# Writing both rounded parts of the residual state in permuted order, so that the gather's stationary chunks are contiguous columns

## The chip, the cores and the metric

The kernel runs on one core of one Trainium2 chip. The metric is the device time of one execution in microseconds (us). It is given as the median of several runs. One further execution was taken by the hardware profiler, and every row shown below comes from that one. The engines are named as the profile names them: PE is TensorE (PEld its weight loads), DVE is VectorE, ACT is ScalarE, POOL is GpSimd, and SP is the engine whose queue issues the weight transfers. A matmul has a stationary operand, which a weight load (LDWEIGHTS) puts into the array first, and a moving operand, which is then streamed through it.

## The reference, cut to what matters

One decoder layer on 256 tokens of width 2048: a norm, a projection, two kinds of attention, an output projection that is added to the residual state `h`, and then a mixture of 32 experts. Only the last part matters here.

```python
h = h + mixed @ w_out[layer]
hn = rms_norm(h, ffn_norm_w[layer])
h = h + hier_moe(hn, ...)

# hier_moe: a router picks 1 of 4 groups and 2 of its 8 experts for each token
for e in range(N_EXPERTS):                       # 32
    he = jax.nn.silu(xf @ w_gate[e]) * (xf @ w_up[e])
    y = y + combine[:, e:e + 1] * (he @ w_down[e])
```

Each expert has three float32 matrices of 4 MB (2048 x 512, 2048 x 512 and 512 x 2048).

## The kernel before

**The residual state.** `xs[t]` holds the state `h` as [128 tokens, 2048 columns] for token block t (0 or 1). For the expert stage it is split into two fp32r tensors, `hh[t][0]` (the rounded value) and `hh[t][1]` (what the rounding left). `split_h(n, eng)` makes columns 512 n to 512 n + 511 of them: two ACT copies (L872) and then two subtractions on the engine `eng` (L874). The first three chunks (n = 0, 1, 2) are split by DVE while the output projection `wo` still runs. The last one (n = 3) is split by POOL, called at L1083, while DVE works through the router's chain of small operations (L1090 to L1160), which ends in the one-hot matrix `s1` (L1065).

**Pairs of experts.** The 32 experts are taken as 16 pairs (`pr` 0 to 15). Each expert gets up to 64 tokens (`CAP`). `gather_j` picks the tokens of two pairs (four experts, 256 places) out of `hh` with matmuls: for chunk j of 512 columns, the stationary operand is a 128 x 128 piece of `hh` and the moving operand is the one-hot matrix `s1` of 256 columns. The weights of an expert are loaded so that partition p holds rows 4p to 4p + 3 of a chunk, so a gather needs for i = 0 to 3 the columns 4q + i of that chunk, q = 0 to 127. Before the change these are read with a step of four elements (16 bytes) out of `hh`, at L1197. One call of `gather_j` is 16 matmuls (4 values of i, 2 token blocks, 2 parts) into two PSUM tiles `bx`, and DVE takes each tile out at L1199 (`xg`).

**What runs when on PE.** The gather for pairs 0 and 1 stands ahead of the loop: chunks j = 0 and 1, then the gate matmuls `bg` of chunk 0, then chunk 2, `bg` of chunk 1, and so on. In the loop over pairs, an odd pair (1, 3, ..., 13) gathers for the next two pairs: a chunk of `gather_j` after each of the four parts of its `up` matmuls (`bu`, in `in_u`). So there are eight gathers of 4 x 16 = 64 matmuls. An even pair has none. After `bu` come the next pair's `bg` and this pair's `by` (down). Each part of `bg`, `bu` or `by` is 16 matmuls on two weight tiles.

**Weights.** All expert weights go through a ring of SBUF slots of 1 MB each: 391 loads in a fixed order on the SP queue (`expert_load`, L958). 20 slots are filled ahead of the expert stage, and in the stage 16 of them are reused in turn. A load waits until PE has finished with the tile that its slot held (`used(2)` after each part).

**The scatter.** `scatter_n` brings a pair's result back to the tokens, matmuls `bo`, and adds it to `y`. At the first pair (`base is None`) `y` is made from `hh`: DVE adds `hh[t][0]` to `bo` (L1280) and POOL adds `hh[t][1]` (L1281), eight times each. Later pairs add to `y` itself (L1283).

Of the kernel before, what the change touches and what calls it, by code (L numbers as in the profile page):

```python
# [11 lines left out]
F32 = mybir.dt.float32  # L12
# [4 lines left out]
ALU = mybir.AluOpType  # L17
# [4 lines left out]
P = 128  # L22
# [58 lines left out]
def tile_kernel(ctx: ExitStack, tc: tile.TileContext, a: dict, out):  # L81
    nc = tc.nc
    pe, act, dve, pool, sp = nc.tensor, nc.scalar, nc.vector, nc.gpsimd, nc.sync
# [26 lines left out]
    def m8(tag, name, shape, dt=F32):  # L110
        return big.tile([P, *shape], dt, tag=tag, name=name)

    def mm(o, l, r, start, stop):
        pe.matmul(o, l, r, start=start, stop=stop, skip_group_check=True)  # L114


    xs = [big.tile([P, D], F32, tag=f"s{t}", name=f"xs{t}") for t in range(2)]
# [746 lines left out]
    hh = []  # L864

    def split_h(n, eng):

        if not hh:
            hh.extend([m8(tag, f"hh{t}{k}", (D,), F32R) for k, tag in enumerate(HH[t])] for t in range(2))
        ns = slice(n * 512, (n + 1) * 512)  # L870
        for t in range(2):
            act.copy(hh[t][0][:, ns], xs[t][:, ns])  # L872
        for t in range(2):
            eng.tensor_tensor(hh[t][1][:, ns], xs[t][:, ns], hh[t][0][:, ns].bitcast(F32), ALU.subtract)  # L874


    def logits(n):
# [22 lines left out]
        if n < 3:  # L900
            yield
            split_h(n, dve)
            for _ in range(3):
                yield
# [72 lines left out]
    for i in range(4):  # L977
# [3 lines left out]
        for kk in range(4):  # L981
            k = 4 * i + kk
# [19 lines left out]
            hi, lo = halves[h]  # L1002
# [78 lines left out]
    act.copy(lgT[0:36, :], ob["lg"][0:36, :T])  # L1081
    act.copy(lgT[64:100, :], ob["lg"][64:100, :T])
    split_h(3, pool)  # L1083
    blg = bank("blt", "s")
    for t in range(2):
# [100 lines left out]
    def gather_j(nm_, xg, s1, j, n):  # L1186

        xt_ = mp.tile([P, 4, 4 * CAP], F32, tag="xg", name=f"xg{nm_}{j}", bufs=4)
        xg.append(xt_)
        m = n * CAP  # L1190
        per = 512 // m
        for i0 in range(0, 4, per):
            bx = psm.tile([P, 512], F32, tag="A", name=f"bx{nm_}{j}{i0}")
            for t in range(2):
                for k in range(2):
                    for i in range(i0, i0 + per):
                        mm(bx[:, (i - i0) * m:(i - i0 + 1) * m], hh[t][k][:, j * 512 + i:(j + 1) * 512:4],  # L1197
                           s1[:, t, 0:n].rearrange("p e c -> p (e c)"), i == i0 and t + k == 0, t + k == 2)
            dve.tensor_tensor(xt_[:, i0:i0 + per, 0:m], bx.rearrange("p (i s) -> p i s", i=per),  # L1199
                              fw[:, 4 * j + i0:4 * j + i0 + per].unsqueeze(2).broadcast_to([P, per, m]), ALU.mult)  # L1200
# [32 lines left out]
    hids, ys, y = [], [], []  # L1233
# [39 lines left out]
    def scatter_n(nm_, scT, n, base):  # L1273
        ns = slice(n * 512, (n + 1) * 512)
        for t in range(2):
            bo = psm.tile([P, 512], F32, tag="A", name=f"bo{nm_}{n}{t}")
            for k in range(2):
                mm(bo, scT[:, t * P:(t + 1) * P], ys[0][:, n % 2, k], k == 0, k == 1)
            if base is None:
                dve.tensor_tensor(y[t][:, ns], hh[t][0][:, ns].bitcast(F32), bo, ALU.add)  # L1280
                pool.tensor_tensor(y[t][:, ns], y[t][:, ns], hh[t][1][:, ns].bitcast(F32), ALU.add)  # L1281
            else:
                dve.tensor_tensor(y[t][:, ns], base[t][:, ns], bo, ALU.add)  # L1283

# [24 lines left out]
    xg = []  # L1309
    bgs = psm.tile([P, 512], F32, tag="GU", name="bg0")  # L1310
    gather_j("0", xg, s1, 0, 4)
    for j in range(4):
        if j < 3:
            gather_j("0", xg, s1, j + 1, 4)
        half_in("0", "g", xg, 0, lambda j, e: wt["g", 0, j, e], lambda: used(2), bgs, (j,))
# [3 lines left out]
    for pr in range(16):  # L1319
# [8 lines left out]
        def in_u(j):  # L1328

            if by is not None and j in (0, 2):  # L1330
                for n in (j, j + 1):
                    scatter_n(str(pr - 1), scT_, n, None if pr == 1 else y)
                if j == 0:
                    split_y(by, 2)
                    split_y(by, 3)
            if more:
                gather_j(str(pr + 1), xg2, s1, j, 4)
# [68 lines left out]
    with tc.If(over >= CAP + 1):  # L1406
        for r in range(1, T // CAP):
            with tc.For_i(0, 32, 2) as e0:
# [31 lines left out]
                for n in range(4):  # L1440
                    split_y(by, n)
                    scatter_n(nm_, scT, n, y)
# [42 lines left out]
```

## Time and profile before

| what | value |
|---|---|
| median of 3 runs | 1439.66 us (1438.49 to 1439.86) |
| the profiled execution: its own time | 1438.52 us |
| the profiled execution: span in the trace | 1436.7 us |
| PE busy | 1366.0 us, 95% of the span |
| DVE, ACT, POOL busy | 503.5, 311.0, 73.5 us |
| read from HBM | 476.63 MB |

The span goes from the first to the last instruction, and the execution's own time has 1.8 us more around it. A busy PE is not a PE at its peak: matmuls overlap one another, and the busy time counts the whole stretch that they cover.

### The profile page before, as it was taken

The numbers are of one execution on the slowest core, as the hardware profiler recorded it, in microseconds if no ns is written. First come the engines' busy times: TensorE is split into PE (matmuls) and PEld (weight loads), VectorE is DVE, ScalarE is ACT, GpSimd is POOL, SyncE is SP. The second block draws the span as 40 slices with busy tenths as digits, with TensorE's granted clock in tenths as the row PEclk, the third lists the DMA queues.
The fourth block names the chain that finished last, engine by engine and source line by source line (L and its number), as shares of the span: only waits on it lengthen the run. The fifth ranks groups of instructions, "written<-read, shape, count | busy, mean of one in ns | idle before, by whom it ended". The sixth has DMA issues, their size and how long they took to land.

```text
span 1436.7 us, 18318 instructions
## 1 busy us (share of the span) xinstructions
PE 1366.0 (95%) x7526; PEld 817.4 (57%) x7526; DVE 503.5 (35%) x1046; ACT 311.0 (22%) x632; POOL 73.5 (5%) x94
## 2 busy tenths in 40 slices
PE   9999999999999999999999998999899899899985
PEld 8999999899787635434434532633543353363332
DVE  4657877767765203013022120310302122031022
ACT  5454545545544000000000000010000000001003
POOL 0300010121100002000000000000000000000003
PEclk9999999999999999999999999999999999999998
DMA  8754344655695799899999999999999999999994
GB/s 274 223 170 146 121 139 129 200 161 164 229 354 210 301 398 408 350 421 421 421 420 421 421 421 421 421 420 421 420 420 421 420 422 420 422 421 421 421 400 153
DMA packets 116698, 480.04 MB, mean 334 GB/s; under 512 B 14368, under 2 KB 40832, under 8 KB 68352
## 3 DMA queue, kind: packets, MB, share of 16 engines
q1 hardware_dynamic: 112240, 474.53, 83.8%
q10 hardware_dynamic: 4368, 4.27, 0.9%
q8 instruction: 61, 1.00, 0.3%
q14 instruction: 29, 0.24, 0.1%
HBM read 476.63 MB, written 2.14 MB: 333 GB/s over the span
## 4 chain that ended last, share of the span: by engine, by line
PE 70%; DMA 22%; DVE 4%; ACT 2%; SPq 1%; issue 1%; ACTq 0%; POOL 0%; DVEq 0%; POOLq 0%
PE bu L114 12%; PE bg L114 10%; PE bx L114 9%; DMA e_d<-in_expert_w_down_dram 8%; DMA e_u<-in_expert_w_up_dram 8%; PE by L114 8%; PE fkv_ps L114 6%; PE wo L114 6%; DMA e_g<-in_expert_w_gate_dram 4%; PE bo L114 3%; PE q_ps L114 3%; PE fq_ps L114 3%; PE o L114 2%; PE kvw_ps L114 2%; PE kvs_ps L114 1%; PE s_n L114 1%
## 5 line engine op out<-in xcount | busy, mean ns | idle before, releaser
L114 PE MATMUL by<-e_d,hids 128*64 128x512 f32 (+2 forms) x1072 | 231.2, 575 | 16.0 <-DMA e_d<-in_expert_w_down_dram 15.3
L114 PE MATMUL bu<-e_u,xg 128*64 128x512 f32 x1024 | 237.2, 596 | 7.5 <-DMA e_u<-in_expert_w_up_dram 7.5
L114 PE MATMUL bg<-e_g,xg 128*64 128x512 f32 x1024 | 226.5, 594 | 0.0
L1271 DVE TENSOR_TENSOR ys<-by,ys 128x512 fp32r<-128x512 f32 x60 | 40.0, 687 | 418.3 <-ACT ys L1270 417.0
L114 PEld LDWEIGHTS by<-e_d,hids 128*64 128x64 f32 x1072 | 79.1, 137 | 163.4 <-issue 127.7
L114 PEld LDWEIGHTS bu<-e_u,xg 128*64 128x64 f32 x1024 | 71.9, 137 | 143.4 <-issue 126.1
L114 PEld LDWEIGHTS bg<-e_g,xg 128*64 128x64 f32 x1024 | 71.7, 137 | 133.8 <-issue 130.5
L114 PEld LDWEIGHTS bx<-s,hh 128*128 128x128 f32 x512 | 122.2, 330 | 23.6 <-issue 13.0
L114 PE MATMUL bx<-s,hh 128*128 128x256 f32 x512 | 128.4, 404 | 4.5 <-DVE y L1283 3.0
L1283 DVE TENSOR_TENSOR y<-y,bo 128x512 f32<-128x512 f32 x112 | 72.0, 684 | 144.2 <-PE bo L114 144.2
L1270 ACT CAST ys<-by 128x512 fp32r<-128x512 f32 x60 | 35.2, 586 | 289.7 <-PE by L114 182.8
L1199 DVE TENSOR_TENSOR xg<-bx,fw 128x512 f32<-128x512 f32 x64 | 44.3, 692 | 134.4 <-PE bx L114 134.4
L114 PE MATMUL bo<-ys,scT 128*128 128x512 f32 x240 | 73.0, 426 | 12.3 <-ACT ys L1270 6.2
L114 PE MATMUL wo<-cv_wo,ohi 128*128 128x512 f32 x256 | 80.6, 396 | 0.0
L114 PEld LDWEIGHTS bo<-ys,scT 128*128 128x128 f32 x240 | 38.0, 188 | 58.7 <-issue 41.5
L1213 ACT CAST scT<-bsc 128x256 fp32r<-128x256 f32 x16 | 6.0, 373 | 250.8 <-PE bsc L114 250.8
L114 PE MATMUL fkv_ps<-xhl,cv_fkv 128*128 128x256 f32 x384 | 59.7, 291 | 0.0
L114 PE MATMUL fkv_ps<-cv_fkv,xhl 128*128 128x256 f32 x384 | 56.3, 282 | 0.0
L1391 POOL TENSOR_TENSOR o<-y,e_fnw 128x256 f32<-128x256 f32 (+2 forms) x12 | 10.1, 868 | 840.9 <-DVE y L1304 840.9
L114 PEld LDWEIGHTS wo<-cv_wo,ohi 128*128 128x128 f32 x256 | 46.9, 188 | 10.4 <-issue 1.2
L188 DVE TENSOR_TENSOR cv_fkv<-raw_fkv,cv_fkv 128x1024 fp32r<-128x1024 f32 x32 | 42.7, 1335 | 28.7 <-ACT cv_fkv L187 28.7
L114 PE MATMUL fq_ps<-xhl,cv_fq 128*128 128x256 f32 x384 | 52.4, 289 | 0.0
(285 smaller groups left out, 1464.8 us busy)
## 6 DMA issues: line engine op xcount, KB each, us to landing
e_g<-in_expert_w_gate_dram SPq DMA_DIRECT2D x128, 1024.0 KB, 19.8
e_u<-in_expert_w_up_dram SPq DMA_DIRECT2D x128, 1024.0 KB, 19.7
e_d<-in_expert_w_down_dram SPq DMA_DIRECT2D x124, 1024.0 KB, 19.8
raw_fkv<-in_w_in_dram SPq DMA_DIRECT2D x32, 512.0 KB, 4.8
raw_wo<-in_w_out_dram SPq DMA_DIRECT2D x16, 1024.0 KB, 5.1
raw_q<-in_w_in_dram SPq DMA_DIRECT2D x8, 1024.0 KB, 5.2
raw_fq<-in_w_in_dram SPq DMA_DIRECT2D x8, 1024.0 KB, 5.0
raw_kvs<-in_w_in_dram SPq DMA_DIRECT2D x4, 1024.0 KB, 7.1
```

Source lines behind the costliest of these rows:

```text
L114: pe.matmul(o, l, r, start=start, stop=stop, skip_group_check=True)
L188: dve.tensor_tensor(lo, r, hi.bitcast(F32), ALU.subtract)
L1199: dve.tensor_tensor(xt_[:, i0:i0 + per, 0:m], bx.rearrange("p (i s) -> p i s", i=per), fw[:, 4 * j + i0:4 * j + i0 + per].unsqueeze(2).bro ...
L1213: act.copy(scT, bt[:, :T])
L1270: act.copy(hi, by[n])
L1271: dve.tensor_tensor(lo, by[n], hi.bitcast(F32), ALU.subtract)
L1283: dve.tensor_tensor(y[t][:, ns], base[t][:, ns], bo, ALU.add)
L1391: (dve if last else pool).tensor_tensor(o[t][:, ns], y[t][:, ns], fnw[:, ns], ALU.mult)
```

## The change

The change writes `hh` in another column order. Within each chunk of 512 columns, column 4q + i of the state goes to place 128 i + q. `split_h` therefore reads `xs` with a step of four elements and writes `hh` contiguously. The gather's stationary chunk i is then the 128 contiguous columns 128 i to 128 i + 127. Where `y` is first made from `hh`, at L1280 and L1281, the order is turned back: `y` and the PSUM tile `bo` are accessed with a step of four elements there, and `hh` contiguously. No instruction is added, removed or moved: on each engine the same instructions with the same sizes stand in the same order, and only the access patterns differ.

```diff
         ns = slice(n * 512, (n + 1) * 512)
-        for t in range(2):
-            act.copy(hh[t][0][:, ns], xs[t][:, ns])
-        for t in range(2):
-            eng.tensor_tensor(hh[t][1][:, ns], xs[t][:, ns], hh[t][0][:, ns].bitcast(F32), ALU.subtract)
+        src = [xs[t][:, ns].rearrange("p (q i) -> p i q", i=4) for t in range(2)]
+        for t in range(2):
+            act.copy(hh[t][0][:, ns].rearrange("p (i q) -> p i q", i=4), src[t])
+        for t in range(2):
+            eng.tensor_tensor(hh[t][1][:, ns].rearrange("p (i q) -> p i q", i=4), src[t],
+                              hh[t][0][:, ns].bitcast(F32).rearrange("p (i q) -> p i q", i=4), ALU.subtract)
...
-                        mm(bx[:, (i - i0) * m:(i - i0 + 1) * m], hh[t][k][:, j * 512 + i:(j + 1) * 512:4],
+                        mm(bx[:, (i - i0) * m:(i - i0 + 1) * m], hh[t][k][:, j * 512 + i * P:j * 512 + (i + 1) * P],
                            s1[:, t, 0:n].rearrange("p e c -> p (e c)"), i == i0 and t + k == 0, t + k == 2)
...
             if base is None:
-                dve.tensor_tensor(y[t][:, ns], hh[t][0][:, ns].bitcast(F32), bo, ALU.add)
-                pool.tensor_tensor(y[t][:, ns], y[t][:, ns], hh[t][1][:, ns].bitcast(F32), ALU.add)
+                hi, lo = (hh[t][k][:, ns].bitcast(F32).rearrange("p (i q) -> p i q", i=4) for k in range(2))
+                yp = y[t][:, ns].rearrange("p (q i) -> p i q", i=4)
+                dve.tensor_tensor(yp, hi, bo.rearrange("p (q i) -> p i q", i=4), ALU.add)
+                pool.tensor_tensor(yp, yp, lo, ALU.add)
```

## Rows read from the trace of the kernel before

**Rows 1.** The page: span, and the chain that ended last, by engine.

```profile
span 1436.7 us, 18318 instructions
...
PE 70%; DMA 22%; DVE 4%; ACT 2%; SPq 1%; issue 1%; ACTq 0%; POOL 0%; DVEq 0%; POOLq 0%
```

**Rows 2.** Windows: busy us (instructions) of each engine, clock, DMA share, GB/s.

```profile
core 0: us, PE busy (x) PEld busy (x) DVE busy (x) ACT busy (x) POOL busy (x), PEclk, DMA share, GB/s
476.00:524.00 48.00, 48.00 (x232) 21.77 (x233) 4.75 (x9) 3.43 (x7) 0.00 (x0) 1.00 0.80 314
524.00:572.00 48.00, 46.70 (x206) 23.56 (x203) 12.47 (x19) 3.03 (x5) 10.02 (x8) 1.00 1.01 421
572.00:592.00 20.00, 19.46 (x104) 9.64 (x102) 2.04 (x3) 1.46 (x5) 0.00 (x0) 1.00 0.71 270
592.00:1385.00 793.00, 752.82 (x3384) 325.21 (x3382) 151.55 (x231) 55.32 (x107) 0.00 (x0) 1.00 1.01 421
```

**Rows 3.** Waits of SP's queue, 476 to 592 us: total us, times, longest.

```profile
SPq L958 <- PE bg L114: 57.0, 10, 15.1
SPq L958 <- PE bu L114: 40.2, 8, 9.8
```

**Rows 4.** The chain in order of time: start us, us, what.

```profile
468.84 7.80 PE bx L114 x32
476.64 3.58 PE bg L114 x16
480.23 3.95 PE bx L114 x16
...
548.97 4.04 PE bx L114 x16
```

**Rows 5.** Weight loads by shape: busy us, mean ns of one, idle before.

```profile
L114 PEld LDWEIGHTS bx<-s,hh 128*128 128x128 f32 x512 | 122.2, 330 | 23.6 <-issue 13.0 <-DVE y L1283 8.1 <-DVE y L1280 1.4
...
L114 PEld LDWEIGHTS fkv_ps<-cv_fkv,xhl 128*128 128x128 f32 x384 | 50.5, 191 | 0.0
...
L893 PEld LDWEIGHTS bt<-cst,xs 128*128 128x128 f32 x32 | 4.9, 207 | 0.9 <-DVE xs L846 0.4
...
L283 PEld LDWEIGHTS xt<-cst,xs 128*128 128x128 f32 x32 | 3.7, 139 | 1.1 <-DVE xhl L285 0.9
```

**Rows 6.** Timeline of PE in the projection: start us, us, operation.

```profile
304.64 0.88 PE L114 MATMUL fkv_ps<-xhl,cv_fkv 128*128 128x256 f32 x6
305.36 0.88 PE L114 MATMUL fkv_ps<-cv_fkv,xhl 128*128 128x256 f32 x6
```

**Rows 7.** Windows again, with the granted clock in the third column from the right.

```profile
461.00:470.00 9.00, 5.86 (x46) 5.62 (x47) 7.15 (x38) 2.04 (x6) 2.49 (x2) 1.00 0.97 380
470.00:474.00 4.00, 4.00 (x19) 4.00 (x19) 1.38 (x2) 0.00 (x0) 0.00 (x0) 0.57 1.01 420
1360.00:1380.00 20.00, 15.65 (x68) 5.31 (x64) 2.62 (x4) 1.76 (x3) 0.00 (x0) 1.00 1.01 422
```

**Rows 8.** Timeline of POOL and DVE at the last split and the router.

```profile
462.21 2.49 POOL L874 TENSOR_TENSOR hh<-xs,hh 128x512 fp32r<-128x512 f32 x2 [1.70 <-ACT hh L872]
...
463.21 1.53 DVE L1100 TENSOR_TENSOR room<-room 128x64 f32<-128x64 f32 x2
...
465.16 0.30 DVE L1107 TENSOR_TENSOR room<-room 128x64 f32<-128x64 f32 x2
```

**Rows 9.** Timeline of POOL at three earlier places.

```profile
46.58 0.72 POOL L480 TENSOR_TENSOR bk<-kc,vec 128x240 f32<-128x240 f32 x1 [7.50 <-DVE kc L336]
...
52.05 4.13 POOL L480 TENSOR_TENSOR bk<-kc,vec 128x240 f32<-128x240 f32 x3 [0.20 <-DVE kc L336]
...
206.27 0.73 POOL L621 TENSOR_TENSOR sq<-sq,s 128x256 f32<-128x256 f32 x1
```

**Rows 10.** DVE and ACT groups by line: busy us, mean ns of one, idle before.

```profile
L1199 DVE TENSOR_TENSOR xg<-bx,fw 128x512 f32<-128x512 f32 x64 | 44.3, 692 | 134.4 <-PE bx L114 134.4
...
L1280 DVE TENSOR_TENSOR y<-hh,bo 128x512 f32<-128x512 f32 x8 | 5.1, 684 | 8.0 <-PE bo L114 8.0
...
L456 DVE TENSOR_TENSOR cb<-bcb,csf 128x120 f32<-128x120 f32 x4 | 0.9, 276 | 1.4 <-PE bcb L114 1.4
...
L872 ACT CAST hh<-xs 128x512 fp32r<-128x512 f32 x8 | 4.5, 611 | 0.0
```

## Prediction

> **What bounds the kernel now.** I read the page first, then windows by stage, then the waits of the load queue and the chain inside the stage that the change touches. The chain that ended last is 70% PE and 22% DMA [rows 1], so both kinds of stretch exist, and the question is in which one a saved microsecond counts. The windows answer it [rows 2]. From 592 to 1385 us the transfers run at 421 GB/s without a break. That is also the rate of the full stretch from 524 to 572 us, so it is the ceiling as this trace shows it. In those 793 us the kernel ends when its bytes have come, and PE time saved there only becomes waiting. Six of the eight gathers lie there.
>
> Before that the transfers are not full. From 476 to 524 us they run at 314 GB/s, and from 572 to 592 us at 270 GB/s [rows 2]. Measured against 421, the first stretch lacks 48 x (421 - 314) / 421 = 12.2 us of transfer, and the second 20 x (421 - 270) / 421 = 7.2 us. Together that is 19.4 us. The reader is to see who withholds them: the load queue waits for PE to give slots back, 57.0 us for `bg` and 40.2 us for `bu` [rows 3]. The first two gathers stand just there (468.84 to 491.7 us, and from 548.97 us on [rows 4]), and they delay each slot's release. So the first two gathers count, and only up to 19.4 us.
>
> **What a contiguous stationary operand is worth.** A weight load of the gather takes 330 ns, and the same shape and type with contiguous columns takes 191 ns in `fkv` [rows 5]. Another pair of rows isolates the step: the transposes of `xs` load 207 ns where they read every fourth column (`bt`) and 139 ns where they read contiguous ones (`xt`) [rows 5]. So I hold the step responsible, not the tensor. Spacing matters more than duration, because loads overlap matmuls. The gather's 512 loads cover 122.2 us without overlap, 239 ns each, and they set the pace. Six `fkv` matmuls with the same stationary and moving sizes start every 305.36 - 304.64 = 0.72 us [rows 6], 120 ns each. I take 119 ns saved per matmul, 1.9 us per call of 16, and 7.6 us per gather. The bounds: nothing, if something else holds the 239 ns, and 7.6 us.
>
> The Trainium skill's page "TensorE: Matmul & The Clock Gate", section "LDWEIGHTS (loading the stationary operand)", gives a load's time by the number of columns alone, for 128 columns about 107 ns; by it the step costs nothing and the sum would be zero. The trace disagrees, 330 against 191 ns [rows 5], so I give that rule little weight.
>
> **First gather.** Its two first calls run back to back, 32 matmuls in 7.80 us [rows 4]. From 470 to 474 us the mean granted clock is 0.57, so 1.2 GHz instead of 2.4 for 0.43 / 0.5 x 4 = 3.4 us, after a router stretch in which PE was busy 5.86 of 9 us [rows 7]. At half clock I double the 120 ns to 240, an estimate, no better than the 239 ns of now. So 3.4 / 0.239 = 14 matmuls gain nothing, and 18 x 0.119 = 2.1 us remain. If the half clock falls elsewhere next time, the two calls gain the full 3.8 us. The calls for j = 2 and 3 gain 1.9 us each. Slots are then freed 2.1, 4.0 and 5.9 us earlier, and from there to the next gather always 5.9 us earlier. The last starved moment of the first stretch lies behind all four calls, so the transfers get 5.9 of the lacking 12.2 us back (7.6 with the clock elsewhere).
>
> **Second gather.** Its four calls save 7.6 us again, on top of the 5.9 by which everything is early. The second stretch lacks only 7.2 us, so PE then frees slots before the queue needs them, and the 7.2 us go whole. From about 520 us on the transfers are full, and nothing further can be won: the remaining six gathers save some 45 us of PE time that turn into waits for transfers.
>
> **What the change may cost.** PSUM hand-over: DVE takes 0.69 us for each `bx` tile [rows 10], now about 1.9 us apart and then 0.96. There are two tiles, and I allow 0.4 us in the first gather for PE waiting on one; in the second it comes out of the 0.4 us by which 7.6 exceeds 7.2.
>
> POOL's last split is the edit that can reach the path. While its two subtractions run (462.21 to 464.70), two small DVE operations take 1.53 us that take 0.30 us elsewhere, and they end with POOL [rows 8]: DVE stands still until POOL is done, and the router's chain, on which the first gather waits, stands behind it. So any lengthening of these two operations moves the whole expert stage. POOL reads with a step here for the first time. Its nearest row is L480, which steps 16 elements in its source: 0.72 us for 240 elements, against 0.73 us for 256 contiguous ones [rows 9]. By that the step costs nothing. The worst L480 row is 4.13 / 3 = 1.38 us, beside DVE work. That is 1.9 times as long, which would add 0.9 x 2.49 = 2.3 us. I take 0.3 us, near the undisturbed row, and keep 0 and 2.3 as ends.
>
> The Trainium skill's page "GPSIMD Engine Reference", section "7. Performance pitfalls for Q7 kernels", says that reading SBUF with a byte step over 8 costs about half as much again. By that rule the two would take 1.2 us more and the sum would be 1.2 us worse; the undisturbed L480 row with its 64-byte step does not show it.
>
> The other edits I cost at nothing. The first six subtractions and six ACT copies of `split_h` lie beside `wo` matmuls on engines with idle time; the last ACT copies (611 ns, [rows 10]) start POOL, so a tenth more there is below 0.1 us. At L1280 DVE reads PSUM with a step; L456 reads it with a step of 16 elements and takes 276 ns for 120 elements, and L1280 takes 684 for 512 [rows 10], both close to 1 ns an element and a fixed part, so the step is free. If it doubled, eight times 0.68 = 5.4 us would stand in the second gather, less what its 7.6 us leave over. L1281's result is wanted only by the next pair's scatter.
>
> **Sum.** 5.9 + 7.2 - 0.4 - 0.3 = 12.4 us; for small stalls that I can't name I round to 12. The profiled execution took 1438.52 us (span 1436.7 [rows 1]), which gives 1426.5; it lies 1.14 us under the median of the runs, so the median after should be 1427.7. I say 1427.5.
>
> **Rivals.** (a) Hidden anyway: transfers at 421 GB/s bind, gain zero, 1439.7 us. For it speaks the long full stretch; against it the 19.4 us lacking before it, which wait for PE by name [rows 3]. 3%. (b) The change doesn't do what it says: the load's time hangs on columns alone (the rule above) or on the tensor, and the spacing stays at 239 ns; 1439.5 to 1442 with POOL's cost. Against it the two pairs of rows. 3%. (c) Partial: the spacing falls only half-way, say 180 ns, or POOL costs its 2.3 us. With 0.94 us saved per call, 1.1 + 1.9 + 3.8 less 0.7 give 6 us, 1433.5. 11%. (d) Slower: with PE faster, its waits for transfers grow by about 45 us, and PE falls to the half clock in them. A part of 16 matmuls then takes up to twice 3.58 us [rows 4], while its two tiles (2.1 MB) come in 5.0 us: each such part loses 2.2 us once no lead is left. Some 160 parts lie in the 793 us; one in ten at half clock would be 16 x 2.2 = 35 us against the 12, so about 1463. It decides from six such parts on. Against it: where PE waits for transfers today it is busy 15.65 of 20 us and the clock stays at 1.00, and the fall came after 5.86 of 9 us [rows 7]. 3%. My forecast keeps 80%.
>
> **How the numbers follow.** With the half clock elsewhere and POOL free the gain is 7.6 + 7.2 = 14.8 us, 1424.9, and the three runs of before spread by 1.4 us: I set 1423.5. The upper end takes in POOL's 2.3 us and most of (c): 1432.5. A measurement of this kernel can tell about 0.2%, 2.9 us, from no change. Faster: the forecast and (c) with little left out, 0.91. Slower: (d) and some of (b), 0.04. Same: the rest, 0.05.
>
> **What the profile after would show.** Weight loads of `bx` near 190 ns; a call of 16 in about 2.1 us instead of 3.95; the transfers at 421 GB/s from about 520 us on, with no second short stretch; the stretch 476 to 524 still short, but by about 6 us; SP's waits for `bg` and `bu` smaller there; more PE waiting for `e_d`, `e_u` and now `e_g` after 700 us with the clock at 1.00; POOL L874 near 1.27 us. A DMA rate that is broken again after 560 us, or POOL L874 at 2 us and more, would make the prediction wrong.

## Result, and the profile after

| kernel | median us | lowest to highest | ratio to before (95%) |
|---|---|---|---|
| before | 1439.08 (4 runs) | 1436.84 to 1439.86 | |
| after the change | 1427.58 (4 runs) | 1426.43 to 1428.56 | 0.9927 [0.9914, 0.9940] |

The change makes the kernel 11.5 us faster. Predicted were 1427.5 us and a gain of 12. The sum came out; some of its terms did not, and the rest of this document is about them. The profiled execution took 1427.72 us, 10.8 us less than the one of the kernel before. Below, "after" is this profile.

The page of the kernel after: its span and the chain that ended last, by engine, against [rows 1].

```profile
span 1425.9 us, 18327 instructions
...
PE 56%; DMA 37%; DVE 4%; ACT 2%; issue 1%; SPq 0%; ACTq 0%; POOL 0%; DVEq 0%; POOLq 0%
```

PE's share of the chain went from 70% to 56%, and DMA's from 22% to 37%: more of the end is now decided by transfers. The groups of the same profile (busy us, mean ns of one, idle before):

```profile
L114 PEld LDWEIGHTS bx<-s,hh 128*128 128x128 f32 x512 | 62.2, 188 | 23.8 <-issue 13.0 <-DVE y L1287 8.1 <-DVE y L1284 1.5
...
L1285 POOL TENSOR_TENSOR y<-y,hh 128x512 f32<-128x512 f32 x8 | 12.1, 1548 | 84.9 <-DVE y L1284 84.9
...
L873 ACT CAST hh<-xs 128x512 fp32r<-128x512 f32 x8 | 8.6, 1120 | 0.0
...
L1284 DVE TENSOR_TENSOR y<-hh,bo 128x512 f32<-128x512 f32 x8 | 7.9, 1080 | 7.5 <-PE bo L114 7.5
```

The weight load fell from 330 [rows 5] to 188 ns. The price stands in the other three rows: ACT's copy rose from 611 to 1120 ns and DVE's first scatter from 684 to 1080 ns [rows 10], and POOL's scatter rose by a fifth from what it was before:

```profile
L1281 POOL TENSOR_TENSOR y<-y,hh 128x512 f32<-128x512 f32 x8 | 10.0, 1288 | 95.9 <-DVE y L1280 95.9
```

The windows, against [rows 2], and one from the part that is bound by transfers:

```profile
core 0: us, PE busy (x) PEld busy (x) DVE busy (x) ACT busy (x) POOL busy (x), PEclk, DMA share, GB/s
476.00:524.00 48.00, 48.00 (x249) 18.98 (x250) 4.75 (x9) 3.43 (x7) 0.00 (x0) 1.00 0.94 368
524.00:572.00 48.00, 45.01 (x240) 20.84 (x238) 17.03 (x22) 3.91 (x9) 12.05 (x8) 1.00 1.01 422
572.00:592.00 20.00, 20.00 (x96) 6.94 (x94) 0.00 (x0) 1.27 (x2) 0.00 (x0) 1.00 0.97 382
592.00:1375.00 783.00, 711.35 (x3342) 288.61 (x3340) 150.45 (x231) 54.62 (x106) 0.00 (x0) 1.00 1.01 421
...
1350.00:1370.00 20.00, 15.65 (x66) 5.33 (x62) 3.07 (x5) 1.85 (x4) 0.00 (x0) 1.00 1.01 421
```

The first stretch now lacks 48 x (421 - 368) / 421 = 6.0 us of transfer instead of 12.2, and the second 20 x (421 - 382) / 421 = 1.9 instead of 7.2. Together 11.5 us came back: the gain in the medians, and 0.7 us more than the 10.8 between the two profiles. The second stretch is still broken, though; the prediction had named a broken rate after 560 us as a sign that it is wrong. From 592 us on nothing changed in the rate. SP's waits in the same two stretches (476 to 592 us) show whom this came from; [rows 3] had 57.0 and 40.2 (its waits for `by` rose, from 10.3 to 12.8 us):

```profile
SPq L960 <- PE bg L114: 50.4, 11, 11.5
SPq L960 <- PE bu L114: 36.7, 8, 8.7
```

The chain through the router and the first two gathers (start us, us, what), against [rows 4]. `room` is the scratch tile of DVE's small operations in the router.

```profile
465.44 2.51 DVE room L1102 x2
...
472.06 4.17 PE bx L114 x32
476.23 3.58 PE bg L114 x16
479.81 2.10 PE bx L114 x16
...
545.63 2.15 PE bx L114 x16
```

A call of 16 matmuls takes 2.10 us instead of 3.95. POOL's last split, which holds DVE at the router, against [rows 8]:

```profile
464.90 3.03 POOL L875 TENSOR_TENSOR hh<-xs,hh 128x512 fp32r<-128x512 f32 x2 [2.19 <-ACT hh L873]
...
465.40 2.55 DVE L1102 TENSOR_TENSOR room<-room 128x64 f32<-128x64 f32 x2
```

It takes 3.03 us instead of 2.49, and it starts later, because ACT's copies feed it.

One profile shows where the gain lies only when it is cut into pieces that both kernels share. `blt` is the router's matmul just ahead of POOL's split. All numbers are us, worked out from starts in the timelines of the two kernels and of a second run of the changed one (`c1_changed_again`, below).

| piece | before | after | c1 |
|---|---|---|---|
| start of the span to `blt` | 461.64 | 463.83 | 459.38 |
| `blt` to the first gather | 7.20 | 8.23 | 8.23 |
| first gather to the first `bu` | 31.42 | 24.10 | 26.21 |
| first `bu` to the end of the second gather | 78.28 | 72.30 | 72.32 |
| end of the second gather | 578.54 | 568.46 | 566.14 |

The first row is chance: c1 runs the same program as after and reaches `blt` 4.45 us earlier. By 460 us it had moved 88.9 MB and after 87.2 (added up from windows of 4 us), which is 4.0 us of transfer at 421 GB/s. The second row is a loss of 1.03 us by the change. The third is where the clock falls by chance, and the fourth is the steady part of the gain, 6.0 us.

### The profile page after: what moved, and what is told of

It is laid out like the page before. It is cut to its first block, busy times and chain, and to the rows that moved or that the text cites. A ratio compares the mean times of both kernels' runs of the same rounds, so it can differ in the third digit from the quotient of the medians.

```text
span 1425.9 us, 18327 instructions
## 1 busy us (share of the span) xinstructions
PE 1321.7 (93%) x7526; PEld 771.5 (54%) x7526; DVE 509.2 (36%) x1046; ACT 315.3 (22%) x632; POOL 75.9 (5%) x94
## 4 chain that ended last, share of the span: by engine, by line
PE 56%; DMA 37%; DVE 4%; ACT 2%; issue 1%; SPq 0%; ACTq 0%; POOL 0%; DVEq 0%; POOLq 0%
DMA e_u<-in_expert_w_up_dram 17%; DMA e_d<-in_expert_w_down_dram 17%; PE bu L114 12%; PE fkv_ps L114 6%; PE wo L114 6%; PE bg L114 4%; PE by L114 4%; PE bo L114 3%; PE q_ps L114 3%; PE fq_ps L114 3%; PE bx L114 3%; DMA e_g<-in_expert_w_gate_dram 3%; PE kcv_ps L114 2%; PE o L114 2%; PE kvw_ps L114 2%; PE kvs_ps L114 2%
## 5 line engine op out<-in xcount | busy, mean ns | idle before, releaser
L114 PE MATMUL bu<-e_u,xg 128*64 128x512 f32 x1024 | 243.9, 597 | 9.7 <-DMA e_u<-in_expert_w_up_dram 9.6
L114 PE MATMUL bg<-e_g,xg 128*64 128x512 f32 x1024 | 234.8, 596 | 12.9 <-DMA e_g<-in_expert_w_gate_dram 12.9
L114 PEld LDWEIGHTS bg<-e_g,xg 128*64 128x64 f32 x1024 | 81.7, 137 | 143.2 <-issue 107.0
L114 PEld LDWEIGHTS bu<-e_u,xg 128*64 128x64 f32 x1024 | 75.6, 136 | 148.3 <-issue 121.5
L114 PEld LDWEIGHTS bx<-s,hh 128*128 128x128 f32 x512 | 62.2, 188 | 23.8 <-issue 13.0
L114 PE MATMUL bx<-s,hh 128*128 128x256 f32 x512 | 68.7, 287 | 4.6 <-DVE y L1287 2.9
L1395 POOL TENSOR_TENSOR o<-y,e_fnw 128x256 f32<-128x256 f32 (+2 forms) x12 | 10.1, 866 | 835.9 <-DVE y L1308 835.9
L114 PEld LDWEIGHTS fkv_ps<-xhl,cv_fkv 128*128 128x128 f32 x384 | 50.3, 190 | 2.2 <-issue 1.2
```

What stands on the lines that cost most here:

```text
L1395: (dve if last else pool).tensor_tensor(o[t][:, ns], y[t][:, ns], fnw[:, ns], ALU.mult)
```

## Experiments

Theory at this point: the first two gathers pay for everything, and the edits at the edges (the splits and the first scatter) cost a few us each time. Rivals: the edges are free, or all eight gathers count. All kernels but the last were timed against the kernel before on the same chip.

**The gather alone.** Splits and scatter stay as before, and the gather reads contiguous columns. The tokens are thus gathered with their columns in another order than the weights expect.

```diff
-  mm(..., hh[t][k][:, j * 512 + i:(j + 1) * 512:4], ...)
+  mm(..., hh[t][k][:, j * 512 + i * P:j * 512 + (i + 1) * P], ...)
```

> Only the gather's stationary chunk is made contiguous; the splits and the first scatter are those of before. hh is not permuted, so the experts get the columns of each chunk in another order than their weights (this part of the computation is changed; the router and the amount of work are not). Theory: the gain lies in the first two gathers, and the stepped accesses of the change cost about 1.0 us at the last split (POOL and ACT, through DVE's stand) and 1.5 us at the first scatter. Without them this kernel gets 6 to 7.3 us back in the first stretch and all of the lacking 7.2 us in the second: 13 to 14.5 us under the kernel before, about 1425.5 us, so 2 us under the changed kernel. L1100's pair stays at 1.5 us. Rival, the stepped accesses cost nothing in the total: 1427.6 us, as the changed kernel.

Measured 1421.89 us, 0.9894 [0.9876, 0.9912]. That is more gain than the whole change gives (0.9928 in c1), so the edges cost about 5 us in the medians. The pieces show 1.0 us at the router (7.21 instead of 8.23) and 1.5 us in the second gather (70.81 instead of 72.30). Against c1 the first gather is shorter as well, 25.60 us instead of 26.21, and the three pieces make 3.1 us, as much as the two profiles' spans differ by (1423.5 and 1420.5 us). The rest is not placed; three of its four executions had a mean clock of 0.995 or 0.996, where the changed kernel's had 0.993 or 0.994, so some of it may be the clock.

**The edges alone.** The mirror image: splits and scatter as after the change, and the gather keeps its step of four. Again the gathered columns are in another order.

```diff
-  mm(..., hh[t][k][:, j * 512 + i * P:j * 512 + (i + 1) * P], ...)
+  mm(..., hh[t][k][:, j * 512 + i:(j + 1) * 512:4], ...)
```

> The splits and the first scatter of the changed kernel, with the stepped stationary chunk of before in every gather (the experts get the columns in another order, the work is the same). Theory: it pays the stepped accesses and gains nothing: 1.0 us later at the first gather, 1.5 us more in the second, both before the transfers are full, so about 2.5 us over the kernel before, 1441.6 us. Rival, the stepped accesses are free in the total: 1439.1 us. Third, the late start of 3.2 us seen after is all due to the change (not to a half clock in the first 20 us of that execution): 4.7 us over, 1443.8 us.

Measured 1439.64 us, 1.0016 [1.0007, 1.0024], a loss of 2.3 us. In its profile `blt` to the first gather takes 8.22 us and the second piece 80.09, against 7.20 and 78.28: 1.0 and 1.8 us. (Its clock was at 0.96 between 524 and 572 us, which is not priced here.) The chain has the gather at its old pace:

```profile
469.51 7.78 PE bx L114 x32
...
480.87 3.95 PE bx L114 x16
```

So the edges do not pay for anything by themselves, and the weight load does not get faster by the new layout alone. The interval's upper end is 1.0024 x 1437.81 - 1437.81 = 3.5 us, which leaves out the dearest of the three prices expected.

**The first two gathers contiguous, the last six stepped.** The six gather columns in another order.

```diff
+  near = nm_ in ("0", "2")
+  st = hh[t][k][:, j*512+i*P:j*512+(i+1)*P] if near else hh[t][k][:, j*512+i:(j+1)*512:4]
-  mm(..., hh[t][k][:, j * 512 + i * P:j * 512 + (i + 1) * P], ...)
+  mm(..., st, ...)
```

> The changed kernel with contiguous stationary chunks in the first two gathers alone; the other six step through hh as before (the experts from pair 4 on get the columns in another order, the work is the same). Theory: the six gathers lie where transfers at 421 GB/s bind, so the time is that of the changed kernel, 1427.6 us within 0.7. Rival, every gather counts alike, about 1.75 us each of 14 before costs: 2 x 1.75 less 2.5 us, so 1438 us.

Measured 1426.68 us, 0.9926 [0.9913, 0.9939]: the changed kernel's time. **The last six contiguous, the first two stepped** is the opposite (`not in`).

> The reverse: contiguous chunks in the last six gathers, stepped ones in the first two (the experts of pairs 0 to 3 get the columns in another order, the work is the same). Theory: no gain, only the cost of the stepped accesses, as in the kernel with the edges alone: about 2.5 us over the kernel before, 1441.6 us, although PE saves some 45 us. Rival, every gather counts alike: 6 x 1.75 less 2.5 us, so 8 us under, 1431 us.

Measured 1440.29 us, 1.0019 [1.0010, 1.0028]: no gain, and the edges' price stays. Two gathers of eight carry the whole gain. What the six do can be read from PE's waits for transfers (total us, times, longest); `e_g`, `e_u` and `e_d` are the weight tiles of gate, up and down. First the kernel with the first two contiguous, 592 to 1375 us:

```profile
PE by L114 <- DMA e_d<-in_expert_w_down_dram: 15.4, 13, 1.3
PE bu L114 <- DMA e_u<-in_expert_w_up_dram: 6.9, 6, 1.3
```

Then the kernel after, the same stretch:

```profile
PE by L114 <- DMA e_d<-in_expert_w_down_dram: 31.8, 24, 1.3
PE bg L114 <- DMA e_g<-in_expert_w_gate_dram: 12.9, 11, 1.3
PE bu L114 <- DMA e_u<-in_expert_w_up_dram: 9.6, 9, 1.3
```

22.3 us of waiting became 54.3, and in the windows of that stretch PE was busy 743.27 us in the one and 711.35 in the other, both with transfers at 421 GB/s. The same 32 us stand in both differences: PE time saved in the six gathers is waiting.

**The changed kernel again**, with the profile taken again, to see what of a profile is chance.

> The changed kernel again, unaltered, beside the three variants below. Ratio to the kernel before 0.992 to 0.993. From the router's blt matmul to the first gather 8.23 us again (7.20 in the kernel before). If the half clock of the first 20 us is by chance and not due to the change, this profile has it or not, with the router stage reached 2 us earlier when not.

Measured 1427.03 us, 0.9928 [0.9914, 0.9941]. Its windows and its chain at the first gather:

```profile
core 0: us, PE busy (x) PEld busy (x) DVE busy (x) ACT busy (x) POOL busy (x), PEclk, DMA share, GB/s
...
466.00:472.00 6.00, 4.63 (x23) 4.52 (x23) 3.56 (x14) 0.00 (x0) 0.00 (x0) 0.50 1.01 421
```

```profile
467.61 6.33 PE bx L114 x32
```

Here the granted clock was 0.50, that is 1.2 GHz, for about 5 of the 6.33 us that the first 32 matmuls took; after had the clock at 1.00 there and took 4.17. What a matmul takes at the low level can be read from the timeline of PE, cut at 469 and at 472 us:

```profile
468.63 5.31 PE L114 MATMUL bx<-s,hh 128*128 128x256 f32 x28
...
471.62 2.33 PE L114 MATMUL bx<-s,hh 128*128 128x256 f32 x14
```

Fourteen matmuls start in 471.62 - 468.63 = 2.99 us, 214 ns each. After had its low clock elsewhere: between 6 and 18 us its mean granted clock was 0.72, against 1.00 in c1.

**POOL's last split behind the router.** POOL's subtractions wait for the router's result, and so do not run beside DVE's chain; the last of the loads that the ring makes ahead move behind them.

```diff
-  split_h(3, pool)
+  split_h(3, pool, (0,))          # ACT's copies only
...
+  gone = mp.tile([P, 1], F32, tag="gone", name="gone", bufs=1)
+  pool.tensor_copy(gone, rc[:, 0, 0, 1:2])
+  split_h(3, pool, (1,))          # POOL's subtractions
```

> The changed kernel, but POOL's last subtractions start only when the router's chain on DVE is done (a one-element POOL copy that reads its last result stands ahead of them); the ring's last loads into xs follow them. Theory: the DVE operation that stood still beside POOL (L1102, 2.51 us for the pair) takes 0.3 us, so from blt to the first gather 6.0 us instead of 8.23, all slots come free 2.2 us earlier, and the total is 2.2 us under the changed kernel, 0.15% (the gather for j = 3 needs this part only 10 us later). Rival: DVE doesn't stand because of POOL, and nothing moves. Second rival: the two last loads into xs start about 3 us later and the gain is lost to the transfers.

Measured 1422.05 us, 0.9893 [0.9878, 0.9908]: some 5 us faster than the changed kernel, twice what was expected. DVE's chain and the first gather in its profile:

```profile
462.26 0.27 DVE room L1102 x2
...
466.69 4.15 PE bx L114 x32
```

The two `room` operations take 0.27 us instead of 2.51, and `blt` to the first gather falls from 8.23 to 6.03: that is 2.2 us, and it shows that POOL's split held DVE. The rest is about the clock. The timeline of PE in the same profile, at the router's last matmuls:

```profile
465.42 0.18 PE L114 MATMUL brk<-sel,lt 128*128 128x32 bf16 x1 [0.28 <-DVE sel L1146]
```

PE waits 0.28 us here; in the two profiles of the changed kernel it waits 2.48 and 2.46 us. The first 32 matmuls then ran at full clock, and the first gather took 24.02 us to the first `bu`, against 26.21 in c1. The mean clock of the runs is 0.995 to 0.996, against 0.993 and 0.994 for the changed kernel. A difference of 0.0025 over 1424 us at half speed is 0.0025 x 1424 / 0.5 = 7 us less at the low level in each execution, an estimate. c1 shows what such a stretch costs when it meets the first gather, 26.21 - 24.02 = 2.2 us. So 2.2 us are shown by the router's piece, and 2.2 more by the first gather of this pair of profiles; that the medians differ by the same cause is argued from the clock.

**The first `y` made ahead.** POOL makes `y` as the sum of the two parts of `hh` ahead of the first scatter, on time that it has to spare, and the first scatter then is like the later ones.

```diff
+  hi, lo = (hh[t][k][:, ns].bitcast(F32).rearrange("p (i q) -> p i q", i=4) for k in range(2))
+  pool.tensor_tensor(y[t][:, ns].rearrange("p (q i) -> p i q", i=4), hi, lo, ALU.add)
...
-  scatter_n(str(pr - 1), scT_, n, None if pr == 1 else y)
+  scatter_n(str(pr - 1), scT_, n, y)
```

> The changed kernel, but POOL adds the two parts into y ahead, while the first pair's down matmuls run, and the first scatter then adds bo to y like all others. Theory: the stepped DVE operation (1080 ns) at the first scatter was on PE's path, 1.5 us in all; the second gather gets them back: from the first bu to the end of the second gather 70.8 us instead of 72.3. The total gains up to 1.5 us, no more than the second stretch still lacks (1.8 us). Rival: the scatter is hidden, no difference.

Measured 1426.31 us, 0.9918 [0.9905, 0.9932]. The profile shows what was meant, 71.05 us from the first `bu` to the end of the second gather instead of 72.32. The ratios of this kernel and of c1 overlap, so its worth in time is not settled. **Both together:**

> Both of the edits above on the changed kernel. Theory: the gains add, 2.2 + 1.5 us: 3 to 4 us under the changed kernel, about 0.990 of the kernel before. Rival: either is hidden, then 2.2 or 1.5 us.

Measured 1423.94 us, 0.9905 [0.9890, 0.9920]. Not better than the split's move alone, and the intervals overlap. Whether the second edit adds anything on top of the first stays open.

**The clock by itself.** Ten more filler matmuls (L1089 of the changed kernel) keep PE busy through the wait at the router, after the change, and five more do so in the kernel before (17 to 22).

```diff
-  keep_clock("clock1", 17)
+  keep_clock("clock1", 27)
```

> The changed kernel with 27 instead of 17 dummy matmuls (their result is not used) beside the router's chain, so that PE is busy for 2.4 us more of the 2.5 us in which it waits for that chain. The first gather starts no sooner: 8.23 us after blt as before. Theory: with PE busy the clock stays at 2.4 GHz at the first gather in most executions, its first 32 matmuls take 4.1 us instead of up to 6.3, and the median is 1 to 2 us under the changed kernel, 1425 to 1426 us against about 1427; the remaining 3 to 4 us to the kernel with the split after the router are the earlier start (2.2 us) and chance. Rival: the clock plays no part, the split after the router gained its 5 us elsewhere, and this kernel takes 1427 us.

Measured 1424.84 us, 0.9918 [0.9904, 0.9931]. In its timeline PE's wait is gone, and in the chain the first 32 matmuls run at full pace:

```profile
467.61 0.18 PE L114 MATMUL brk<-sel,lt 128*128 128x32 bf16 x1 [0.23 <-DVE sel L1146]
```

```profile
468.88 4.15 PE bx L114 x32
```

But this execution had its low clock between 6 and 18 us (0.86), as after had, and after ran these matmuls at full pace without the filler. So this profile alone does not tell whether the filler did it, and in time it is 1.4 us against c1 with intervals that overlap. The profiles of all kernels together say more. In nine of them PE waits 1.46 to 2.48 us in front of `brk`, and eight of these have the low clock during the first gather; after is the ninth. In the other five (the two with filler and the three with the split moved) the wait is 0.23 to 0.35 us, and the clock is 1.00 there in all. What that is worth in the medians is not settled.

> The kernel before with 22 instead of 17 dummy matmuls at the same place (its router is 1 us shorter, so fewer fit). Theory: with stepped chunks a gather matmul takes 234 to 239 ns at either clock, so the clock at the first gather is worth nothing there: same as before within 0.1%. Rival: a half clock costs the kernel before as much as the changed one, then 1 to 2 us under before.

Measured 1436.36 us, 1.0000 [0.9989, 1.0010]. This profile has the clock at full around the router. The 32 matmuls take 7.75 us, against 7.80 [rows 4], and the first gather takes 31.36 us to the first `bu`, as it took 31.42 with the fall in it. So a stepped gather does not gain from the higher clock: 239 ns per matmul holds at either level.

**The split behind the router, again:**

> The changed kernel with POOL's last subtractions after the router's chain, unaltered from the earlier run. Ratio 0.988 to 0.991 to the kernel before again; from blt to the first gather 6.0 us, PE's wait for the router 0.3 us, and the first 32 gather matmuls in 4.1 us if the clock stays up.

Measured 1422.02 us, 0.9896 [0.9881, 0.9911]. It agrees with the first time. Its low clock fell at neither place, and the first gather took 24.08 us to the first `bu`. This version beats both kernels, the kernel before by 15 us.

**What a step costs, operand by operand** (one execution, for its profile). Chunk 1 of the splits reads contiguously and writes with a step of 512 bytes, chunk 2 uses a step of 8 bytes, and the others use 16. In the first scatter one operand at a time is stepped. Some chunks of `hh` and `y` so have another column order.

```diff
-  act.copy(hh...rearrange("p (i q) -> p i q", i=4), src[t])
+  act.copy(w(hh[t][0][:, ns]), v(xs[t][:, ns]))      # v, w by chunk
...
+  f = {0: (even, even, step), 1: (step, even, even), 2: (even, step, even), 3: (step, even, step)}[n]
+  dve.tensor_tensor(f[0](yn), f[1](hi), f[2](bo), ALU.add)
+  pool.tensor_tensor(f[0](yn), f[0](yn), f[1](lo), ALU.add)
```

> The changed kernel with other stepped operands in each of the four chunks, to price each by itself (columns come in another order, the work is the same). Split: chunks 0 and 3 read xs with a step of 16 bytes as in the changed kernel; chunk 1 reads contiguously and writes hh with a step of 512 bytes; chunk 2 reads with a step of 8 bytes. First scatter on DVE: chunk 0 steps (16 bytes) in PSUM alone, chunk 1 in y's write alone, chunk 2 in hh's read alone, chunk 3 as in the changed kernel; POOL alike. Theory, from L456 (PSUM step of 64 bytes at no cost) and the 1072 ns of the split: it is the SBUF read at 16 bytes that costs: split chunk 2 near 684 ns on DVE, PSUM alone near 684, hh's read alone near 1080, y's write alone unknown, near 1080 as chunk 3 has no stepped SBUF read on DVE. Rival: any stepped operand costs the same.

The timeline of this kernel, on ACT and DVE two operations in each row: chunks 0 (16-byte read), 1 (512-byte write) and 2 (8-byte read) of the splits, then DVE's scatter with only the PSUM operand stepped and with only `y` stepped. Then POOL's, one operation in each row: no step in SBUF, and `hh` read with a step.

```profile
424.26 2.13 ACT L879 CAST hh<-xs 128x512 fp32r<-128x512 f32 x2
...
437.40 2.08 ACT L879 CAST hh<-xs 128x512 fp32r<-128x512 f32 x2
...
446.80 1.23 ACT L879 CAST hh<-xs 128x512 fp32r<-128x512 f32 x2
```

```profile
425.53 2.07 DVE L881 TENSOR_TENSOR hh<-xs,hh 128x512 fp32r<-128x512 f32 x2
...
438.66 2.12 DVE L881 TENSOR_TENSOR hh<-xs,hh 128x512 fp32r<-128x512 f32 x2
...
448.74 1.28 DVE L881 TENSOR_TENSOR hh<-xs,hh 128x512 fp32r<-128x512 f32 x2
...
540.93 1.29 DVE L1292 TENSOR_TENSOR y<-hh,bo 128x512 f32<-128x512 f32 x2 [3.90 <-PE bo L114]
542.50 2.02 DVE L1292 TENSOR_TENSOR y<-hh,bo 128x512 f32<-128x512 f32 x2 [0.29 <-PE bo L114]
```

```profile
541.75 1.30 POOL L1293 TENSOR_TENSOR y<-y,hh 128x512 f32<-128x512 f32 x1 [77.83 <-DVE y L1292]
...
556.86 1.55 POOL L1293 TENSOR_TENSOR y<-y,hh 128x512 f32<-128x512 f32 x1 [9.58 <-DVE y L1292]
```

On DVE a step of 8 bytes in SBUF is free (1.28 us for two, where one without a step takes 684 ns), one of 16 or 512 bytes costs some 0.4 us for 512 elements, a write costs as much as a read (2.02 us for two with `y` written with the step, 2.04 with `hh` read), and a step of 16 bytes in PSUM is free (1.29). ACT is alike in SBUF. Two stepped operands cost no more than one: in chunk 1 DVE reads and writes `hh` with the step (2.12 us for two), in chunk 0 only `xs` is stepped (2.07). On POOL a stepped read costs 0.25 us. A stepped write alone does not: in the kernel that makes `y` ahead, POOL reads `hh` contiguously, writes `y` with the step, and takes 1287 ns.

The Trainium skill's page "Advanced Engine Details and Errata", section "Memory Cachelines", says that SBUF has lines of 16 bytes and needs two hits on a line to hide its latency. The rows on DVE and ACT agree: with 8 bytes two elements share a line, with 16 none do.

## Why the prediction was right, and where it was not

**What bounds the kernel: right.** The transfers' shortfall before 592 us was to be the store of the gain, and 11.5 us of it came back for 11.5 us of time. The other profiles bear it out. What each had moved by 592 us (added up from windows of 4 us), as time at 421 GB/s, is ahead of the kernel before by 9.4 us in after, 12.1 in c1, 14.8 with the gather alone and 16.0 in the last run with the split moved; their spans are shorter by 10.8, 13.2, 16.2 and 16.6 us. Contiguous chunks in the first two gathers alone give 0.9926, in the last six 1.0019.

**The weight load: right.** 188 ns against "near 190", 2.10 us a call against "about 2.1", so 7.4 us a gather against 7.6. The rule that a load's time hangs on the columns alone (the Trainium skill, "TensorE: Matmul & The Clock Gate", section "LDWEIGHTS (loading the stationary operand)") would have left the load's time as it was. The kernel with the edges alone (329 ns, new layout, stepped) and the one with the gather alone (193 ns, old layout, contiguous) leave it no room here, since the time follows the columns' step. Rival (b) falls with it. Why a step costs the load that much was not tried.

**First gather: right in both cases, by its own condition.** Predicted 5.9 us, or 7.6 with the low clock elsewhere. With the low clock in it (c1) it is 31.42 - 26.21 = 5.2, without it (after) 7.3. That the half clock is no better than 239 ns was nearly so: the doubled 120 ns are 214 in c1, worth 25 ns a matmul that the prediction left out. That the stepped gather loses nothing by the fall was assumed in it and is now measured (7.75 us at full clock against 7.80).

**Second gather: over-sized.** "The 7.2 us go whole" failed: the second stretch still lacks 1.9 us. What it missed is DVE's first scatter, costed at nothing from L456. That row has its step in PSUM, which is free; the dear operand is `y` in SBUF, and L1280 has both. 684 became 1080 ns, and the second gather takes 1.5 us longer by it (72.30 against 70.81 us with the old scatter). PE's waits between 496 and 582 us (total us, times, longest), before and after, show most of that:

```profile
PE bo L114 <- DVE y L1280: 0.4, 1, 0.4
```

```profile
PE bo L114 <- DVE y L1284: 1.6, 2, 0.8
```

With the gather alone, whose scatter is the old one, the transfers run at 410 GB/s from 572 to 592 us, and the stretch lacks 0.5 us. The prediction had named the price of a doubling, 5.4 us, but had put it all on the PSUM side.

**PSUM hand-over, 0.4 us: not seen.** Calls of 16 take 2.10 us, and the two calls back to back 4.17, less than twice that.

**POOL's split: under-sized.** Taken at 0.3 us with 2.3 as the end, and it is 1.03. Half of it is POOL (2.49 to 3.03 us), half ACT, whose copies start POOL (POOL's idle time before it went from 1.70 [rows 8] to 2.19 us): "a tenth more" became 611 to 1120 ns each. L480 was the wrong row for POOL: it steps in SBUF too and shows no cost, and why it does not (it differs by a repeated second input and runs of 15 elements) stays open. The Trainium skill's page "GPSIMD Engine Reference", section "7. Performance pitfalls for Q7 kernels", had about half as much again for a byte step over 8. The direction was right, and the trace shows 22% (1267 to 1547 ns), so the rule's 1.2 us stands against 0.54 us here. The copies and splits beside `wo` cost nothing, as said: from the first `wo` matmul to `blt` it is 104.2 us in every kernel.

**So the sum held by errors that cancel.** The second gather was taken 1.2 us too high and POOL's split 0.7 too cheap; against that stand the 0.4 for a hand-over that was not needed and the first gather, which after ran at full clock and so 1.4 us better than the term in the sum. With the terms as they came out in after: 7.3 - 1.03 + 6.0 = 12.3 us to the end of the second gather, less 2.2 us by which it reached the router later, which is chance, gives 10.1 us there (578.54 to 568.46), and 10.8 us in the span. In c1, with the fall at the other place: 5.2 - 1.03 + 6.0 = 10.2, plus 2.3 by an earlier start, 12.4, and 13.2 us in the span. The prediction's 12 lies between the two; that the median met 1427.5 to 0.1 us is luck.

**After 592 us.** PE's waits for `e_d`, `e_u` and `e_g` grew as said, at a clock of 1.00, by 32 us rather than some 45 (against the kernel with the first two gathers contiguous). For the 15.65 busy of 20 us near the end the clock stayed at 1.00, and rival (d) did not show. Rivals (a) and (c) fall with the time. The six gathers did save the 45 us: from 592 to 1375 us the `bx` matmuls are busy for 51.6 us in after and for 96.4 in that kernel. But `bu`, `by` and `bg`, with the same number of matmuls within two and the same mean duration within half a per cent, are busy for 600.7 us instead of 582.0, so they stand further apart. (The groups overlap, so these sums do not add up to the 32.) That the gaps between them are waits for transfers too is argued, not shown.

## What to carry to other kernels

A change in layout moves a price from the engine that reads often to those that write and read once. Cost each of those edges by a row whose step lies in the same memory, on the same engine and with the same bytes, and look first at the ones on the path. Time saved on PE counts only where the transfers wait for PE: read that from the load rate by stretch, and check it by making only those stretches faster. One profile can hold 2 to 4 us of chance on either side of a step, so take a second one of the same kernel before explaining a few us.

## What the runs showed of the hardware

- A weight load of 128 x 128 fp32r takes 188 to 195 ns from contiguous columns and 330 ns with a step of 16 bytes. The stepped gather runs at 239 ns per matmul at either clock level; the contiguous one at about 120 ns at the high level and 214 at the low one.
- DVE stood still behind POOL's split: two operations that take 0.27 us together took 2.51 beside it. The Trainium skill's page "SBUF — State Buffer", section "SBUF: two separate sides", has this as an exclusive lock between a DVE operation with two inputs in SBUF and a POOL operation that reads SBUF. The trace agrees, and moving the split gave 2.2 us back.
- The low clock falls now at the start (between 6 and 18 us) and now at the router, in executions of one program (at both in two profiles of other kernels), and what it costs depends on what runs then. After a wait of PE of 2.46 us in front of `brk` c1 ran its first gather at 0.50; after ran it at 1.00 behind the same wait of 2.48 us. Why it fell in the one and not in the other stays open; of the three profiles with the split moved, which have a wait of 0.28 us there, none shows it at the router.
- Prices of a step of 16 bytes in SBUF for 512 fp32 elements: ACT 611 to 1120 ns, DVE 684 to 1080 ns, whether read or written; POOL 1288 to 1548 ns, for reads alone.
